# Seven-product FFN tiles: one 512-column matmul where two 256-column matmuls shared a weight half

## The chip, the cores and the metric

The kernel runs on one core of a Trainium2 chip. The metric is device time in microseconds (us) of one execution; lower is better. A core has TensorE (PE in the profile: matmul, PEld: weight load), VectorE (DVE), ScalarE (ACT), GpSimd (POOL) and SyncE (SP), each with its own queue of instructions, and 16 DMA engines.

## The reference, cut to what matters

One decoder layer on 512 tokens of width 2048: a mixer half (RMSNorm, an input projection, four groups of mixers, an output projection, residual), then a gated MLP, residual, and a final RMSNorm. The change lies in the first matmul of the MLP:

```python
def conv_gated_mlp(h, w_up, w_dw, b_dw, w_down):
    up = h @ w_up                          # (512, 2048) @ (2048, 11008)
    gate, val = jnp.split(up, 2, axis=-1)  # 5504 columns each: 43 tiles of 128
    gate = causal_dwconv(gate, w_dw, b_dw) # width 3
    return (jax.nn.gelu(gate, approximate=True) * val) @ w_down
```

All is float32, and the matmul units are fed with two-part numbers: `hi` is the value rounded to the matmul's format (float32r), `lo` what is left. A product is then hi·hi + hi·lo + lo·hi, three matmuls.

## The kernel before, in words

The work is transposed: a result tile has 128 columns of the weight as its partitions and tokens along its free dimension. `FFN` has 43 tiles `f` of 128 gate columns and the 128 value columns that belong to them. The first three are done plainly (`ffn_std`). The other 40 are done in `ffn_up` by a scheme of the Strassen kind: gate and value, the two halves of the 2048 inputs and the two halves of the 512 tokens make a 2x2x2 product, for which seven products of half the tokens do instead of eight. The seven weight forms of a tile are `a`, `b`, `d` (blocks of the weight as they are), `r1`, `r2`, `r3`, `r4` (sums of blocks); the seven forms of the input lie in the tiles `X0` to `X7`, each `[128, 7, 2, 256]`: form, hi or lo, 256 tokens.

`ffn_up` goes through a list `seq` of products. For each tile from `f` = 4 on the order is: `a` of `f`, `d` of `f`-1, `r1` of `f`, `r4` of `f`-1, `r2` of `f`, `b` of `f`, `r3` of `f`. I call these seven in a row one round. For entry `k` of the list the code writes, in this order:

- `load(k + 6)`: weight blocks from memory by SP's queue (`a`, `b`, `d`); for `r1` and `r3` a block by SP and a second one added to it by a DMA of POOL's queue.
- `stage(k + 2)`: for `r2` and `r4` a sum on VectorE; then the split of the 128x1024 weight form: a ScalarE cast to `hi` (tile `uh...`) and a VectorE subtraction for `lo` (tile `ul...`). The pool `wq` has three buffers for each, so the cast of one product waits for the end of the product three places before.
- `product(k)`: for each of eight input tiles, weight `hi` with input `hi`, weight `hi` with input `lo`, weight `lo` with input `hi`, all into the same 256 columns of a PSUM bank.
- `after(k)`: what the result of the product is used for. Bank "a" of a tile takes `a`, then `r2`, then `r3`, then `d` on top of one another, and bank "r1" takes `r1`, then `r4`. A partial sum that is needed must therefore be read before the next product is added: after `a` and `r2` a copy on ScalarE (tiles `A12`/`A13`), after `r3` a copy to `A14`, to which VectorE adds bank "r1". After `r4` follows the chain that finishes the tile: VectorE makes the gate `g` (`A8`/`A9`), multiplies it by the RMSNorm factor (`rstd`, `A15`), ScalarE and VectorE do the convolution and the gelu into `c` (`A10`/`A11`), VectorE multiplies by the value parts (bank "a" and `A14`), and `keep` sends `c` to memory by SP's queue.

The order on PE is that of the code. On the other queues the builder's scheduler sets the order by its own estimate of the times, with `load` and `stage` raised in priority; once built, each engine takes its instructions in that fixed order.

Of the kernel before, what the change touches and what calls it, by code (L numbers as in the profile page):

```python
# [8 lines left out]
F32 = mybir.dt.float32  # L9
# [4 lines left out]
ADD, SUB, MUL = ALU.add, ALU.subtract, ALU.mult  # L14

P = 128
# [32 lines left out]
class Kernel:  # L49
# [988 lines left out]
    def tail(self):  # L1038
        tc = self.tc
        self.mp.release()  # L1040
        self.ap.release()
        fx = tc.alloc_tile_pool(name="fx", bufs=1, reuse_waits="tile")
        ft = tc.alloc_tile_pool(name="ft", bufs=1, reuse_waits="tile")
        ft2 = tc.alloc_tile_pool(name="ft2", bufs=2, reuse_waits="tile")
        self.x2d = [self.dr.tile([P, 1024], F32, name=f"x2d{p}") for p in range(8)]
        self.tp = ft
        self.acc = self.tmp("rstd", pool=self.cp)
        self.xf = []
        for q in range(4):
            ps = self.quad(q, (0, 2), 0)  # L1050
            for o in range(4):
                x = self.x2[4 * q + o]
                self.tt(x, x, ps[o], ADD)
            for p in (2 * q, 2 * q + 1):
                self.forms1(fx, p)
            for p in (2 * q, 2 * q + 1):
                self.square2(p, ft2)
        self.ffn_std()
        ft2.release()
        ft.release()  # L1060
        self.ffn_up(self.xf, self.rp, self.rs)
        for pool in (fx, self.aq, self.rp):
            pool.release()
        with tc.tile_pool(name="sr", bufs=1, side="right", reuse_waits="tile") as sr, \
                tc.tile_pool(name="sr2", bufs=2, side="right", reuse_waits="tile") as sr2, \
                tc.tile_pool(name="xp", bufs=1, reuse_waits="tile") as xp, \
                tc.tile_pool(name="sp", bufs=1, reuse_waits="tile") as sp, \
                tc.tile_pool(name="dp", bufs=1, reuse_waits="tile") as dp, \
                tc.tile_pool(name="dp2", bufs=2, reuse_waits="tile") as dp2:
            self.tp, self.xp, self.sp, self.sr = dp, xp, sp, sr  # L1070
            base_tmp = self.tmp
            self.tmp = lambda tag, w=512, dt=F32, pool=None: base_tmp(tag, w, dt, pool or {"sq": dp2, "av": sr2}.get(tag))
            self.down()
# [91 lines left out]

    def ffn_up(self, xf, rp, rstd):
        tc, nc, a = self.tc, self.nc, self.a
        IX = {"a": 0, "b": 1, "r4": 2, "r1": 3, "r2": 4, "r3": 5, "d": 6}  # L1170
        seq = [(NSTD, x) for x in ("a", "r1", "r2", "b", "r3")]
        for f in range(NSTD + 1, NF + 1):
            for form, back in (("a", 0), ("d", 1), ("r1", 0), ("r4", 1), ("r2", 0), ("b", 0), ("r3", 0)):
                if f - back < NF:
                    seq.append((f - back, form))
        raws, staged = {}, {}
        blk = self.blk
        v8 = lambda t: t.rearrange("p (k c)->p k c", k=8)

        def raw(f, form):  # L1180
            pool = self.wp if form == "d" else rp
            t = pool.tile([P, 1024], F32, tag="raw", name=f"u{form}_{f}")
            raws[f, form] = t
            return t

        def load(k):
            if k >= len(seq):
                return
            f, form = seq[k]
            if form in ("a", "b", "d"):  # L1190
                nc.sync.dma_start(v8(raw(f, form)), blk(f, form))
            elif form in ("r1", "r3"):
                t = raw(f, form)
                nc.sync.dma_start(v8(t), blk(f, "c"))
                nc.gpsimd.dma_start(v8(t), blk(f, "d" if form == "r1" else "a"), accum_op=ADD)  # L1195

        def stage(k):
            if k >= len(seq) or k in staged:
                return
            f, form = seq[k]  # L1200
            if form == "r2":
                self.tt(raw(f, form), raws[f, "r1"], raws[f, "a"], ADD)
            if form == "r4":
                self.tt(raw(f, form), raws[f, "r2"], raws[f, "b"], ADD)
            hi = self.wq.tile([P, 1024], F32R, tag="hi", name=f"uh{form}_{f}")
            lo = self.wq.tile([P, 1024], F32R, tag="lo", name=f"ul{form}_{f}")
            self.split_to(hi, lo, raws[f, form])
            staged[k] = (hi, lo)

        bank, sv = {}, {}  # L1210

        def product(k):
            f, form = seq[k]
            wh, wl = staged.pop(k)
            new = form in ("a", "b", "r1")
            if new:
                bank[f, form] = self.pa() if form == "b" else self.pb() if f % 2 else self.pa()
            ps = bank[f, {"a": "a", "r2": "a", "r3": "a", "d": "a", "b": "b", "r1": "r1", "r4": "r1"}[form]]
            for p in range(8):
                x, c = xf[p][:, IX[form]], slice(p * P, p * P + P)  # L1220
                self.mm(ps[:, 0:256], wh[:, c], x[:, 0], new and p == 0, False, True)
                self.mm(ps[:, 0:256], wh[:, c], x[:, 1], False, False, True)
                self.mm(ps[:, 0:256], wl[:, c], x[:, 0], False, p == 7, True)

        def after(k):
            f, form = seq[k]
            if form == "a":
                sv[f, "s"] = self.at(12 + f % 2, F32)
                nc.scalar.copy(sv[f, "s"][:, 0:256], bank[f, "a"][:, 0:256])
            elif form == "r2":  # L1230
                nc.scalar.copy(sv[f, "s"][:, 256:512], bank[f, "a"][:, 0:256])
            elif form == "r3":
                sv[f, "w"] = w = self.at(14, F32)[:, 0:256]
                nc.scalar.copy(w, bank[f, "a"][:, 0:256])
                self.tt(w, bank[f, "r1"][:, 0:256], w, ADD)
            elif form == "b":
                sv[f, "g"] = self.at(8 + f % 2, F32)
                self.tt(sv[f, "g"][:, 0:256], bank[f, "b"][:, 0:256], sv[f, "s"][:, 0:256], ADD)
            elif form == "r4":
                g, c = sv[f, "g"], self.at(10 + f % 2, F32)  # L1240
                self.tt(g[:, 256:512], bank[f, "r1"][:, 0:256], sv[f, "s"][:, 256:512], ADD)
                self.tt(g, g, rstd, MUL)
                self.conv_gelu(f, g, c)
                self.stt(c, c, -1.0, rstd, MUL, MUL)
                self.tt(c[:, 0:256], bank[f, "a"][:, 0:256], c[:, 0:256], MUL)
                self.tt(c[:, 256:512], sv[f, "w"], c[:, 256:512], MUL)
                self.keep(f, c)

        LD, AH = 6, 2
        for k in range(LD):  # L1250
            with tc.high_priority(self.hp):
                load(k)
        for k in range(AH):
            with tc.high_priority(self.hp):
                stage(k)
        for k in range(len(seq)):
            with tc.high_priority(self.hp):
                load(k + LD)
                stage(k + AH)
            product(k)  # L1260
            after(k)
# [195 lines left out]
```

## Time and profile before

| | |
|---|---|
| median of 3 runs | 1925.88 us (1922.14 to 1925.94) |
| profiled execution, its own time | 1925.42 us |
| its span in the profile | 1923.6 us |
| busy: PE, PEld, DVE, ACT, POOL | 98%, 88%, 68%, 42%, 9% |
| stage of the 40 seven-product tiles | about 619 to 1431 us |
| chain that ended last, on PE | 89% |
| DMA, mean over the span | 153 GB/s |

Busy time is the share of the span in which an engine had an instruction at work; matmuls overlap each other, so a busy PE is not yet a PE at its peak. The chain is followed back from the last instruction to what released each step. PEclk is the clock that was granted to TensorE, as a share of full speed. In the rows of the profile buffer numbers are left out: `pa` and `pb` are PSUM banks, `uhr`/`ulr` are hi and lo of any of `r1` to `r4`, `A` any of `A8` to `A15`. L96 is the matmul helper, L59 and L62 the VectorE helpers, L105 the cast of a split, L72 an activation.

### The profile page before, as it was taken

The page shows a single profiled execution, that of the slowest core. Times are in us where ns is not written, and L with a number is a line of the kernel's source. Part 1 is how long each engine was busy: PE and PEld are TensorE (multiplying, and loading weights), DVE is VectorE, ACT ScalarE, POOL GpSimd, SP SyncE. Part 2 cuts the span into 40 slices and gives each one's busy share as a digit, 9 for nine tenths or more (in the row PEclk, how much of TensorE's full clock was granted, in tenths as well). Part 3 has the DMA queues.
Part 4 walks back from the last instruction along what each step waited for, and adds up shares of the span by engine and source line. Part 5 has one row for each costly group of instructions (what it writes and reads, how often), then busy time and mean ns, then how long its engine had stood idle before and what let it go on. Part 6 is the DMA issues. An engine that isn't in the chain of part 4 may idle for free.

```text
span 1923.6 us, 29377 instructions
## 1 busy us (share of the span) xinstructions
PE 1875.6 (98%) x11662; PEld 1683.5 (88%) x11662; DVE 1313.1 (68%) x1978; ACT 808.5 (42%) x1054; POOL 164.5 (9%) x243
## 2 busy tenths in 40 slices
PE   8999999999999999999999999999999999999996
PEld 6788887888777999999999999999988888888886
DVE  8699989999683776777767767777774333333334
ACT  6323446432662444544444444444453222222332
POOL 6210020202000000000000000000000000000000
PEclk9999999999999999999999999999999999999998
DMA  5232332533335777777777777777748343333324
GB/s 203 89 96 91 102 93 79 168 102 92 120 125 181 200 195 208 186 194 199 194 211 181 197 202 189 210 186 194 196 126 271 116 139 109 116 110 96 97 95 152
DMA packets 104251, 293.87 MB, mean 153 GB/s; under 512 B 14960, under 2 KB 21104, under 8 KB 104112
## 3 DMA queue, kind: packets, MB, share of 16 engines
q1 hardware_dynamic: 91200, 248.20, 38.7%
q0 software_dynamic: 12624, 43.26, 13.6%
q8 instruction: 91, 1.49, 0.3%
q10 hardware_dynamic: 288, 0.52, 0.1%
q14 instruction: 48, 0.39, 0.1%
HBM read 269.79 MB, written 19.66 MB: 150 GB/s over the span
## 4 chain that ended last, share of the span: by engine, by line
PE 89%; DVE 6%; DMA 2%; ACT 2%; issue 1%; POOL 0%; DVEq 0%; SPq 0%; ACTq 0%; POOLq 0%
PE pa L96 57%; PE pb L96 31%; DVE lo L59 1%; DMA ur<-w_up 1%; ACT hi L105 1%; DVE X L59 1%; DMA av<-act 1%; DVE M L59 0%; DVE bk L59 0%; DMA raw<-w_dnt 0%; ACT L72 0%; DVE l_x L62 0%; DVE A L59 0%; DVE pr L59 0%; DVE A L62 0%
## 5 line engine op out<-in xcount | busy, mean ns | idle before, releaser
L96 PE MATMUL pa<-A,hi 128*128 128x512 f32 x1312 | 414.5, 398 | 14.9 <-ACT A L72 7.3
L59 DVE TENSOR_TENSOR lo<-raw,hi 128x1024 fp32r<-128x1024 f32 (+1 forms) x187 | 231.0, 1236 | 275.9 <-ACT hi L105 275.7
L105 ACT CAST hi<-raw 128x1024 fp32r<-128x1024 f32 (+1 forms) x187 | 195.6, 1047 | 503.9 <-PE pa L96 423.9
L96 PEld LDWEIGHTS pa<-A,hi 128*128 128x128 f32 x1312 | 247.7, 191 | 74.4 <-ACT A L72 7.7
L105 ACT CAST uhr<-ur 128x1024 fp32r<-128x1024 f32 x160 | 167.6, 1047 | 262.0 <-PE pb L96 129.0
L59 DVE TENSOR_TENSOR ulr<-ur,uhr 128x1024 fp32r<-128x1024 f32 x160 | 195.5, 1222 | 116.9 <-ACT uhr L105 116.9
L96 PE MATMUL pa<-A,lo 128*128 128x512 f32 x656 | 258.9, 398 | 2.9 <-DVE lo L59 2.9
L96 PE MATMUL pb<-X,uhr 128*128 128x256 f32 x1280 | 233.9, 283 | 2.0 <-ACT uhr L105 2.0
L96 PE MATMUL pa<-X,uhr 128*128 128x256 f32 x1280 | 233.8, 283 | 0.0
L96 PEld LDWEIGHTS pb<-X,uhr 128*128 128x128 f32 x1280 | 199.7, 192 | 2.2 <-ACT uhr L105 2.2
L96 PEld LDWEIGHTS pa<-X,uhr 128*128 128x128 f32 x1280 | 199.7, 192 | 0.0
L96 PE MATMUL pb<-X,ulr 128*128 128x256 f32 x640 | 181.2, 283 | 0.8 <-DVE ulr L59 0.8
L96 PE MATMUL pa<-X,ulr 128*128 128x256 f32 x640 | 181.1, 283 | 0.0
L96 PEld LDWEIGHTS pa<-A,lo 128*128 128x128 f32 x656 | 124.9, 191 | 32.4 <-DVE lo L59 3.8
L96 PE MATMUL pa<-Sh,hi 128*128 128x512 f32 (+1 forms) x392 | 149.6, 382 | 2.9 <-DVE A L59 2.9
L96 PE MATMUL pa<-Sh,lo 128*128 128x512 f32 (+1 forms) x392 | 149.3, 381 | 0.0
L96 PE MATMUL pa<-Sl,hi 128*128 128x512 f32 (+1 forms) x392 | 149.1, 380 | 0.0
L1195 POOL DMA_DIRECT2D ur<-w_up x80 | 69.9, 874 | 838.7 <-DMA ur<-w_up 276.8
L96 PE MATMUL pb<-Sh,hi 128*128 128x512 f32 (+1 forms) x328 | 125.3, 382 | 0.0
L96 PE MATMUL pb<-Sh,lo 128*128 128x512 f32 (+1 forms) x328 | 125.1, 381 | 0.0
L96 PE MATMUL pb<-Sl,hi 128*128 128x512 f32 (+1 forms) x328 | 124.9, 381 | 0.0
L96 PEld LDWEIGHTS pb<-X,ulr 128*128 128x128 f32 x640 | 122.9, 192 | 1.0 <-DVE ulr L59 1.0
(295 smaller groups left out, 3524.3 us busy)
## 6 DMA issues: line engine op xcount, KB each, us to landing
ur<-w_up SPq DMA_DIRECT2D x80, 512.0 KB, 6.7
ur<-w_up POOLq DMA_DIRECT2D x80, 512.0 KB, 7.9
raw<-w_dn SPq DMA_DIRECT2D x54, 512.0 KB, 3.6
raw<-w_b SPq DMA_DIRECT2D x40, 512.0 KB, 3.7
ud<-w_up SPq DMA_DIRECT2D x40, 512.0 KB, 8.2
ua<-w_up SPq DMA_DIRECT2D x40, 512.0 KB, 6.8
ub<-w_up SPq DMA_DIRECT2D x40, 512.0 KB, 3.7
raw<-w_out SPq DMA_DIRECT2D x32, 512.0 KB, 3.6
```

The lines of the kernel that those rows point to most:

```text
L59: (eng or self.nc.vector).tensor_tensor(out, x, y, op=op)
L96: self.nc.tensor.matmul(ps, lhsT=l, rhs=r, start=start, stop=stop, skip_group_check=go_on)
L105: self.nc.scalar.copy(hi, src)
L1195: nc.gpsimd.dma_start(v8(t), blk(f, "d" if form == "r1" else "a"), accum_op=ADD)
```

## The change

The two matmuls with the same weight half become one of 512 columns: input hi and lo lie side by side in `X`, so weight `hi` meets both at once. Columns 0 to 255 of the bank then hold hi·hi, columns 256 to 511 hold hi·lo, and weight `lo` with input `hi` is added to the latter. Each partial result has now two halves that must still be added. This is done on VectorE, two quarters at a time, in two new tiles of a new pool `ub` with one buffer each: `ut` (for the gate) and `uv` (for the value), each `[128, 2, 2, 256]`.

```diff
-                self.mm(ps[:, 0:256], wh[:, c], x[:, 0], new and p == 0, False, True)
-                self.mm(ps[:, 0:256], wh[:, c], x[:, 1], False, False, True)
-                self.mm(ps[:, 0:256], wl[:, c], x[:, 0], False, p == 7, True)
+                self.mm(ps, wh[:, c], x.rearrange("p n c->p (n c)"), new and p == 0, False, True)
+                self.mm(ps[:, 256:512], wl[:, c], x[:, 0], False, p == 7, True)
+
+        two = lambda t: t.rearrange("p (n c)->p n c", n=2)
+        quad = lambda tag, f: ub.tile([P, 2, 2, 256], F32, tag=tag, name=f"{tag}_{f}")

         def after(k):
             f, form = seq[k]
             if form == "a":
                 sv[f, "s"] = self.at(12 + f % 2, F32)
-                nc.scalar.copy(sv[f, "s"][:, 0:256], bank[f, "a"][:, 0:256])
+                nc.scalar.copy(sv[f, "s"], bank[f, "a"])
             elif form == "r2":
-                nc.scalar.copy(sv[f, "s"][:, 256:512], bank[f, "a"][:, 0:256])
+                sv[f, "u"] = self.at(14, F32)
+                nc.scalar.copy(sv[f, "u"], bank[f, "a"])
             elif form == "r3":
-                sv[f, "w"] = w = self.at(14, F32)[:, 0:256]
-                nc.scalar.copy(w, bank[f, "a"][:, 0:256])
-                self.tt(w, bank[f, "r1"][:, 0:256], w, ADD)
+                sv[f, "v"] = v = quad("uv", f)
+                nc.scalar.copy(v[:, 1], two(bank[f, "a"]))
+                self.tt(v[:, 1], two(bank[f, "r1"]), v[:, 1], ADD)
             elif form == "b":
-                sv[f, "g"] = self.at(8 + f % 2, F32)
-                self.tt(sv[f, "g"][:, 0:256], bank[f, "b"][:, 0:256], sv[f, "s"][:, 0:256], ADD)
+                sv[f, "t"] = quad("ut", f)
+                self.tt(sv[f, "t"][:, 0], two(bank[f, "b"]), two(sv[f, "s"]), ADD)
+            elif form == "d":
+                v = sv[f, "v"]
+                nc.scalar.copy(v[:, 0], two(bank[f, "a"]))
+                self.tt(v[:, :, 0], v[:, :, 0], v[:, :, 1], ADD)
             elif form == "r4":
-                g, c = sv[f, "g"], self.at(10 + f % 2, F32)
-                self.tt(g[:, 256:512], bank[f, "r1"][:, 0:256], sv[f, "s"][:, 256:512], ADD)
+                t, v, g, c = sv[f, "t"], sv[f, "v"], self.at(8 + f % 2, F32), self.at(10 + f % 2, F32)
+                self.tt(t[:, 1], two(bank[f, "r1"]), two(sv[f, "u"]), ADD)
+                self.tt(two(g), t[:, :, 0], t[:, :, 1], ADD)
                 self.tt(g, g, rstd, MUL)
                 self.conv_gelu(f, g, c)
                 self.stt(c, c, -1.0, rstd, MUL, MUL)
-                self.tt(c[:, 0:256], bank[f, "a"][:, 0:256], c[:, 0:256], MUL)
-                self.tt(c[:, 256:512], sv[f, "w"], c[:, 256:512], MUL)
+                self.tt(two(c), v[:, :, 0], two(c), MUL)
                 self.keep(f, c)
```

In `tail` the pool `ub` is opened before `ffn_up` and closed after it. Nothing else is edited. The scheduler orders the queues of the stage anew. In the rows below the digits after a tile's name are its tile `f` and a running number, and a wait names the engine whose semaphore is waited for.

On PE the round of `f` = 22, at the step from `a` of 22 to `d` of 21, read before:

```order
L96 MATMUL pa694_9904<-X7_4972,ula_22_9834 128x256
L96 MATMUL pb687_9669<-X0_4693,uhd_21_9866 128x256 [waits Activation_49]
L96 MATMUL pb687_9669<-X0_4693,uhd_21_9866 128x256
L96 MATMUL pb687_9669<-X0_4693,uld_21_9867 128x256 [waits DVE_49]
L96 MATMUL pb687_9669<-X1_4698,uhd_21_9866 128x256 x2
```

and reads now:

```order
L96 MATMUL pa693_8932<-X7_4972,uha_22_8877 128x512
L96 MATMUL pa693_8932<-X7_4972,ula_22_8878 128x256
L96 MATMUL pb686_8749<-X0_4693,uhd_21_8902 128x512 [waits Activation_49]
L96 MATMUL pb686_8749<-X0_4693,uld_21_8903 128x256 [waits DVE_49]
L96 MATMUL pb686_8749<-X1_4698,uhd_21_8902 128x512
```

In both, `d` goes to the bank that `r3` of 21 was added to, and its first matmul waits for ScalarE.

On ScalarE, the same place in the round before (L1234 is the copy after `r3` of 21, L1229 the copy after `a` of 22):

```order
L105 CAST uhr1_22_9900<-ur1_22_9761 128x1024 [waits DMASW7_49,PE_49]
L1234 COPY A14_693_9894<-pb687_9669 128x256 [waits DVE_49,PE_49]
L105 CAST uhr4_21_9935<-ur4_21_9933 128x1024 [waits PE_49,Activation_49]
L1229 COPY A12_695_9929<-pa694_9904 128x256 [waits PE_49]
L105 CAST uhr2_22_9967<-ur2_22_9965 128x1024 [waits PE_49,Activation_49]
```

and now (L1240 is the copy after `r3` of 21, L1234 that after `a` of 22, L1247 the new one after `d` of 21, L72 the gelu of 20):

```order
L105 CAST uhr1_22_8928<-ur1_22_8819 128x1024 [waits DMASW7_49,PE_49,Activation_49]
L72 ACTIVATE A10_690_8843<-A10_690_8843 128x512 [waits DVE_49,Activation_49]
L105 CAST uhr4_21_8955<-ur4_21_8953 128x1024 [waits PE_49]
L1234 COPY A12_694_8949<-pa693_8932 128x512 [waits PE_49]
L1240 COPY uv_21_8922<-pb686_8749 128x512 [waits DVE_49]
L105 CAST uhr2_22_8981<-ur2_22_8979 128x1024 [waits PE_49,Activation_49]
L1247 COPY uv_21_8922<-pb686_8749 128x512 [waits PE_49]
```

The copy after `r3` stood ahead of the cast for `r4` and of the copy after `a`; it now stands behind both.

On VectorE, the end of the chain of tile 20 before (the two products into `A10`, then the sum into `A14` that follows the copy after `r3` of 21):

```order
L62 SCALAR_TENSOR_TENSOR A10_690_9792<-A10_690_9792,A15_538_4991 128x512 [waits Activation_49]
L59 TENSOR_TENSOR uld_21_9867<-ud_21_9728,uhd_21_9866 128x1024 [waits DMAHW5_49,Activation_49]
L59 TENSOR_TENSOR A10_690_9792<-pa680_9434,A10_690_9792 128x256 [waits DVE_49]
L59 TENSOR_TENSOR A10_690_9792<-A14_686_9659,A10_690_9792 128x256
L59 TENSOR_TENSOR ulr1_22_9901<-ur1_22_9761,uhr1_22_9900 128x1024 [waits PE_49,Activation_49]
L59 TENSOR_TENSOR A14_693_9894<-pb689_9736,A14_693_9894 128x256 [waits Activation_49]
L59 TENSOR_TENSOR ulr4_21_9936<-ur4_21_9933,uhr4_21_9935 128x1024 [waits PE_49,Activation_49]
```

and now (the product with `uv_20` is the last step of tile 20, and the last reader of that buffer):

```order
L62 SCALAR_TENSOR_TENSOR A10_690_8843<-A8_689_8842,par_84,A10_690_8843 128x510 [waits DVE_49]
L59 TENSOR_TENSOR ulr1_22_8929<-ur1_22_8819,uhr1_22_8928 128x1024 [waits PE_49,Activation_49]
L62 SCALAR_TENSOR_TENSOR A10_690_8843<-A10_690_8843,A15_538_4991 128x512 [waits Activation_49]
L59 TENSOR_TENSOR ulr4_21_8956<-ur4_21_8953,uhr4_21_8955 128x1024 [waits PE_49,Activation_49]
L59 TENSOR_TENSOR A10_690_8843<-uv_20_8739,A10_690_8843 128x512 [waits DVE_49]
L59 TENSOR_TENSOR uv_21_8922<-pb688_8802,uv_21_8922 128x512 [waits Activation_49]
L59 TENSOR_TENSOR ulr2_22_8982<-ur2_22_8979,uhr2_22_8981 128x1024 [waits PE_49,Activation_49]
```

The last product of tile 20 stood ahead of the subtractions for `r1` of 22 and `r4` of 21; it now stands behind both. On ScalarE this order holds in the rounds of `f` = 5 to 42 and on VectorE in those of 5 to 41; in round 42 the last product of tile 40 stands ahead of the subtraction for `r4` of 41. On SP only the stores of finished tiles move, by two places, and on POOL nothing moves.

More of the change, by code (lines that the diff above doesn't have):

```diff
@@ L1060, in tail @@
         ft.release()
-        self.ffn_up(self.xf, self.rp, self.rs)
-        for pool in (fx, self.aq, self.rp):
+        ub = tc.alloc_tile_pool(name="ub", bufs=1, reuse_waits="tile")
+        self.ffn_up(self.xf, self.rp, self.rs, ub)
+        for pool in (ub, fx, self.aq, self.rp):
             pool.release()
@@ L1161, in keep, with ffn_up @@
         self.actd.append(t)
-    def ffn_up(self, xf, rp, rstd):
+    def ffn_up(self, xf, rp, rstd, ub):
         tc, nc, a = self.tc, self.nc, self.a
```

## The prediction

> **What bounds the kernel now.** I read the page's busy times first, then its slices.
>
> ```profile
> PE 1875.6 (98%) x11662; PEld 1683.5 (88%) x11662; DVE 1313.1 (68%) x1978; ACT 808.5 (42%) x1054; POOL 164.5 (9%) x243
> ...
> PE   8999999999999999999999999999999999999996
> PEld 6788887888777999999999999999988888888886
> DVE  8699989999683776777767767777774333333334
> ...
> PEclk9999999999999999999999999999999999999998
> ```
>
> TensorE has hardly a gap, and the stage of seven products (slices 13 to 30) has none. So the price of a product is the spacing of its matmuls. The busy times by stage give the spacings, and two products read out in order of time give the shape (columns of the stage rows: window, its length, PE, PEld, DVE, ACT, POOL busy, clock, DMA share, GB/s).
>
> ```profile
> 1000.00:1200.00 200.00, 200.00 (x1669) 200.00 (x1669) 147.03 (x178) 96.93 (x120) 17.29 (x20) 1.00 0.74 197
> ...
> 1600.00:1800.00 200.00, 200.00 (x881) 165.16 (x881) 66.00 (x71) 49.24 (x56) 0.00 (x0) 1.00 0.33 102
> ```
>
> ```profile
> 1000.06 0.40 PE L96 MATMUL pa<-X,uha 128*128 128x256 f32 x2
> ...
> 1002.82 0.28 PE L96 MATMUL pa<-X,ula 128*128 128x256 f32 x1
> 1002.94 0.40 PE L96 MATMUL pb<-X,uhd 128*128 128x256 f32 x2
> ```
>
> A product is 24 matmuls of 256 columns in 1002.94 - 1000.06 = 2.88 us: 120 ns each, and no wait between `a` and `d`. A round of seven takes 20.16 us, 40 of them 806 us. In the later stage, where all matmuls have 512 columns, the spacing is 200/881 = 227 ns: less than twice 120, so a matmul carries about 13 ns beside its columns.
>
> **The matmuls.** Per input tile, three matmuls (360 ns) become one of 512 and one of 256 (227 + 120 = 347 ns). That is 13 ns for 40 x 7 x 8 = 2240 input tiles: -29 us. No row mixes the widths; the bounds are 0 (360 ns stay) and 40 ns for each input tile (the 512 at the price of 320 - 120 = 200), -90 us. I take the spacings as they stand. A product becomes 2.78 us, a round 19.4 us. The Trainium skill ("TensorE: Matmul & The Clock Gate", Back-to-back issue gap) gives N/2.4 + 2.5 ns for an isolated gap, by which a matmul saved would be worth 2.5 ns and the term -6 us; the rows here say 120 ns where this gives 109, so I keep the rows.
>
> **The added work on VectorE and ScalarE.**
>
> ```profile
> L59 DVE TENSOR_TENSOR A<-pa,A 128x256 f32<-128x256 f32 x100 | 42.0, 420 | 12.7 <-PE pa L96 12.5
> L59 DVE TENSOR_TENSOR x<-x,pa 128x512 f32<-128x512 f32 x48 | 32.3, 682 | 1.1 <-PE pa L96 0.8
> ...
> L1229 ACT COPY A<-pa 128x256 f32<-128x256 f32 x20 | 7.3, 366 | 0.0
> L242 ACT COPY A<-pb x1: 586/586/586, 568.9 to 568.9; 128x512 f32<-128x512 f32 x1
> ```
>
> For each tile three sums widen (682 - 420 = 0.26 us each), two sums of 512 are new, and one product of 0.68 replaces two of 0.42: 0.79 + 1.36 - 0.16 = +2.0 us on VectorE. From 147/200 x 20.16 = 14.8 us a round it goes to 16.8 of 19.4 us: 87%, still not the bound. ScalarE gains 3 x 0.22 + 0.59 = 1.2 us on 9.8. As mere load I cost both at nothing: TensorE's 19.4 us a round hide them. DMA moves the same bytes (share 0.74, at 19.4 us at most 0.77); the stores that move on SP wait for a product that a store waited for before, and the loads behind them are issued six products, 6 x 2.78 = 16.7 us, ahead. The order is another matter.
>
> **The new wait.** `d` adds to the bank that `r3` of its tile left, so it must wait for the copy after `r3`. By the new order that copy stands on ScalarE behind the cast for `r4` and the copy after `a`. The cast needs a buffer that frees when `a` ends, and `a` ends exactly where `d` should begin. So the copy cannot run before `d` is due. It has a second condition: its target `uv` has one buffer, whose last reader is the final product of the tile before, and this stands on VectorE behind the subtraction for `r4`, which needs the same cast. The chain from the end of `a`, priced by rows of before:
>
> ```profile
> 1003.08 1.05 ACT L105 CAST uhr<-ur 128x1024 fp32r<-128x1024 f32 x1 [1.24 <-PE pa L96]
> 1004.03 0.37 ACT L1229 COPY A<-pa 128x256 f32<-128x256 f32 x1
> ...
> 1001.29 1.22 DVE L59 TENSOR_TENSOR ulr<-ur,uhr 128x1024 fp32r<-128x1024 f32 x1
> 1002.42 0.42 DVE L59 TENSOR_TENSOR A<-pb,A 128x256 f32<-128x256 f32 x1
> 1004.16 1.23 DVE L59 TENSOR_TENSOR ulr<-ur,uhr 128x1024 fp32r<-128x1024 f32 x1 [1.31 <-ACT uhr L105]
> 1012.24 0.69 DVE L59 TENSOR_TENSOR A<-A,A 128x512 f32<-128x512 f32 x1
> 1021.12 0.42 DVE L59 TENSOR_TENSOR A<-A,A 128x256 f32<-128x256 f32 x1
> 1021.63 0.38 ACT L1234 COPY A<-pa 128x256 f32<-128x256 f32 x1 [0.27 <-DVE A L59]
> ```
>
> - end of `a` to cast: 1003.08 - 1002.94 = 0.14
> - cast to the start of its subtraction: 1004.16 - 1003.08 = 1.08
> - subtraction to the next VectorE instruction: 1002.42 - 1001.29 = 1.13
> - the final product, 128x512: 0.69
> - its end to the copy that waited for it: 1021.63 - 1021.54 = 0.09
> - the copy from the bank, 128x512: 0.59
> - copy to matmul: 0.05, from the rows below
>
> That is 3.77 us by which `d` starts late. ScalarE's own queue alone (cast, copy after `a`, copy after `r3`: 0.14 + 0.95 + about 0.55, a little under its own time, + 0.59 + 0.05) would give 2.3 us, the lower bound. The other inputs are earlier. In VectorE's new queue the subtraction for `r1` starts 0.14 + 1.08 = 1.22 us after the start of `a` (the twelve instructions from the sum after `r4` to it take about 9.4 of the 8.3 + 1.2 us there are), and the multiplication by the norm behind it ends at 1.22 + 1.13 + 0.68 = 3.0; the subtraction for `r4` can start only at 2.78 + 1.22 = 4.0. And the later products find their halves split: each has two products' time for a cast and a subtraction (2.2 us). So nothing pays the wait back. The last tile of before, where `r3` and `d` are neighbours, shows that `d` does wait for such a copy behind a cast:
>
> ```profile
> 1423.50 1.04 ACT L105 CAST hi<-raw 128x1024 fp32r<-128x1024 f32 x1 [1.83 <-PE pa L96]
> 1424.45 0.37 ACT L1234 COPY A<-pa 128x256 f32<-128x256 f32 x1
> ...
> 1423.30 0.28 PE L96 MATMUL pa<-X,ulr 128*128 128x256 f32 x1
> 1424.87 0.50 PE L96 MATMUL pa<-X,uhd 128*128 128x256 f32 x2 [1.29 <-ACT A L1234]
> ```
>
> The copy ended at 1424.82, `d` started at 1424.87, 1.45 us after the 1423.42 at which it was due. In the new order 37 rounds (`d` of 4 to 40) have the whole chain: 139.5 us. `d` of 41 has ScalarE's part, 2.3, and `d` of 42 about 0.6 more than its 1.45 (its copy now also waits for a product of VectorE). Together +142 us.
>
> **The clock after the wait.** A row of 3.4 us each, at three stalls of before:
>
> ```profile
> core 0: us, PE busy (x), PEclk, DMA share, GB/s
> 497.40:500.80 3.40, 1.81 (x7) 1.00 0.24 43
> 500.80:504.20 3.40, 2.88 (x7) 0.53 0.30 114
> ...
> 623.70:627.10 3.40, 1.79 (x12) 1.00 1.04 229
> 627.10:630.50 3.40, 3.40 (x31) 1.00 0.84 295
> ...
> 1436.10:1439.50 3.40, 0.78 (x3) 1.00 0.71 236
> 1439.50:1442.90 3.40, 3.40 (x10) 0.52 0.45 144
> ```
>
> The clock goes in steps of 3.4 us: where TensorE was busy 0.78 or 1.81 of them, the next 3.4 us run at half clock; at 1.79 elsewhere not. So the limit lies near 1.6 us of idle in a step. A wait of 3.77 us leaves 3.6 us idle (the last matmul runs 0.16 into it), spread over two steps. If the first has under 1.6 of it (1.6 of 3.4 positions), the second has over 2.0, and the step after runs at half clock, full of work: 1.7 us lost. If both have over 1.6 (0.4 of 3.4), about 2.5. If the first has over 2.0 (1.4 of 3.4), the half step begins in the idle time: 0.9 to 1.6, mean 1.25. Mean 0.80 + 0.29 + 0.51 = 1.6 us; the ends are 0 and 2.5. Times 37, and about 1 for `d` of 41: +60 us.
>
> The Trainium skill (same page, HAM oscillation — how this bites in real kernels) says that idle gaps over about 3.4 us, a whole window of its monitor, bring half clock. By that this term would be near 4 us in place of 60. The trace here differs: the idle time that ended at 1438.72 was 2.93 us. It stays as a rival.
>
> **The hand-over to the next stage.**
>
> ```profile
> 1438.72 0.50 PE L96 MATMUL pa<-Sh,hi 128*128 128x512 f32 x1 [2.93 <-DVE A L59]
> ```
>
> Before, the next stage's last banks wait for the final product of tile 42, which reads bank "a": 2.9 us, and 1.7 us of half clock behind it (1439.50 above). Now a copy empties that bank earlier, but bank "r1" is read behind splits of the next stage. Between 0 and -4.6 us; I take -3, since the copy has no long chain ahead of it.
>
> **The sum.** -29 + 142 + 60 - 3 = +170 us on the profiled execution's 1925.4: 2095 us. The median of the runs is 0.5 above it: 2096.
>
> **The rivals.**
>
> - Half clock only after a wholly idle step. 3.6 us of idle cover a whole step of 3.4 in 0.2/3.4 = 6% of positions: 37 x 0.06 x 1.7 = 4 us in place of 60, 2040. For it speaks the row at 623.70, where two gaps of a step did nothing; against it 500.80 and 1439.50. 13%. (The Trainium skill's rule above is of this kind.)
> - The shorter wait: if VectorE's final product comes ahead in time of what I worked out, ScalarE's queue alone holds `d` by 2.3 us, 2.1 of them idle; with the limit above two positions in three bring a half step, 1.15 us on average. 37 x (2.3 + 1.15) = 128 in place of 199: 2025. Against it: the subtraction for `r4` has no way past the cast. 8%.
> - Faster: `d` doesn't wait, because the copy after `r3` gets done during `a`, for instance since the order of the built program doesn't hold on the chip. Then -29 - 3: 1893. It decides at a copy done 3.8 us earlier than I have it. The order of before is found in its trace instruction by instruction, so 5%.
> - VectorE's 87% turns into a further wait behind each round, or both steps fall under the limit each time (37 x 2.5 = 92): 2128 or a little more. 9%.
>
> My forecast keeps 65%. The range takes in the shorter wait and the double step: 2022 to 2132. A measurement of this kernel tells about 0.2% from no change; faster 0.05, within it 0.01, slower 0.94.
>
> **What will show it.** Right: the waits list has TensorE waiting for the L1240 copy, about 37 times and 3.6 us each, some 135 us; rows of matmuls 347 ns apart in pairs between; a clock of about 0.93 in the stage, which takes some 980 us; `d` alone starts late. Wrong: no such wait (then the order or the bank's reuse was misread), a clock of 1.00, pairs at 360 ns, or TensorE waiting for VectorE's splits.

## The result, and the profile after

The changed kernel takes 2115.59 us (median of 4 runs, 2114.25 to 2120.2) where the kernel before takes 1924.91 us (4 runs, 1922.14 to 1925.94): a ratio of 1.1001, 95% interval 1.0984 to 1.1019, or 191 us more. The forecast was 2096 us within 2022 to 2132. The direction and the mechanism were right; the size was 20 us short, and the experiments below find in which term.

The page of the changed kernel, busy times and two of the slices:

```profile
PE 1935.1 (92%) x9422; PEld 1621.8 (77%) x9422; DVE 1394.0 (66%) x2018; ACT 851.2 (40%) x1094; POOL 167.1 (8%) x243
...
PE   8999999999998888888888888888889999999997
...
PEclk9999999999999889999999999888999999999998
```

TensorE has 2240 matmuls fewer and is busy for longer: part of its work now runs at half clock. Its row of slices, full before, has 8s through the stage of seven products, slices 13 to 30. The list of waits (what waited, for what: us in all, times, longest) says what is in them:

```profile
PE pa L96 <- ACT uv L1240: 68.2, 20, 3.5
PE pb L96 <- ACT uv L1240: 65.0, 19, 3.5
```

The windows of the stage, with the columns as in the prediction:

```profile
800.00:1000.00 200.00, 172.01 (x878) 147.51 (x877) 132.84 (x150) 84.36 (x103) 14.00 (x16) 0.90 0.59 157
1000.00:1200.00 200.00, 172.00 (x886) 147.78 (x885) 133.58 (x151) 85.28 (x104) 13.54 (x16) 0.91 0.58 157
```

TensorE waits 39 times, 133.2 us, for the copy after `r3` (L1240). VectorE is busy 67% of the stage and ScalarE 42%: neither is the bound by its load. Here is one wait in order of time, on all engines, from the changed kernel's trace:

```profile
1013.16 0.28 PE L96 MATMUL pb<-X,ula 128*128 128x256 f32 x1
...
1013.36 1.05 ACT L105 CAST uhr<-ur 128x1024 fp32r<-128x1024 f32 x1 [0.62 <-PE pb L96]
1014.31 0.58 ACT L1234 COPY A<-pb 128x512 f32<-128x512 f32 x1
1014.44 1.23 DVE L59 TENSOR_TENSOR ulr<-ur,uhr 128x1024 fp32r<-128x1024 f32 x1 [0.69 <-ACT uhr L105]
1015.58 0.68 DVE L59 TENSOR_TENSOR A<-uv,A 128x512 f32<-128x512 f32 x1
...
1016.30 0.59 ACT L1240 COPY uv<-pa 128x512 f32<-128x512 f32 x1 [1.41 <-DVE A L59]
...
1016.94 0.59 PE L96 MATMUL pa<-X,uhd 128*128 128x512 f32 x1 [3.50 <-ACT uv L1240]
...
1017.54 0.63 PE L96 MATMUL pa<-X,uhd 128*128 128x512 f32 x1
...
1018.18 0.63 PE L96 MATMUL pa<-X,uhd 128*128 128x512 f32 x1
```

`a` ends at 1013.16 + 0.12 = 1013.28, the spacing of a 256-column matmul after its start. Cast for `r4`, its subtraction, final product of the tile before, copy after `r3`, `d`: each row begins where the one ahead of it releases it, and `d` is 1016.94 - 1013.28 = 3.66 us late. Behind it come pairs of a 512- and a 256-column matmul 0.64 us apart (1017.54 to 1018.18) in place of 0.35: half clock.

The full waits run from the first to the last of these two rows, 37 of them:

```profile
662.40 0.79 PE L96 MATMUL pa<-X,uhd 128*128 128x512 f32 x1 [3.50 <-ACT uv L1240]
...
1574.23 0.79 PE L96 MATMUL pa<-X,uhd 128*128 128x512 f32 x1 [3.50 <-ACT uv L1240]
```

A round takes 911.83/36 = 25.33 us. At full clock the pairs of this trace are 349 ns apart on the mean (1908 of them). So 7 x 8 pairs are 19.57 us of the round, the wait is 3.66, and 2.10 us are left for the clock, where the forecast had 1.6.

### The profile page after: what moved, and what is told of

It is laid out like the page before. It is cut to its first block, busy times and chain, and to the rows that moved or that the text cites. A ratio compares the mean times of both kernels' runs of the same rounds, so it can differ in the third digit from the quotient of the medians.

```text
span 2112.9 us, 24908 instructions
## 1 busy us (share of the span) xinstructions
PE 1935.1 (92%) x9422; PEld 1621.8 (77%) x9422; DVE 1394.0 (66%) x2018; ACT 851.2 (40%) x1094; POOL 167.1 (8%) x243
## 4 chain that ended last, share of the span: by engine, by line
PE 84%; DVE 8%; ACT 4%; DMA 2%; issue 1%; SPq 0%; DVEq 0%; ACTq 0%; POOLq 0%
PE pa L96 54%; PE pb L96 30%; DVE ulr L59 2%; ACT uhr L105 2%; DVE A L59 1%; DVE lo L59 1%; ACT uv L1240 1%; DMA ur<-w_up 1%; ACT hi L105 0%; DMA raw<-w_a 0%; DVE M L59 0%; DVE X L59 0%; DMA raw<-w_dnt 0%; DMA par<-par 0%; DVE bk L59 0%
## 5 line engine op out<-in xcount | busy, mean ns | idle before, releaser
L96 PE MATMUL pb<-X,uhr 128*128 128x512 f32 x640 | 229.8, 398 | 1.0 <-ACT uhr L105 1.0
L96 PE MATMUL pa<-X,uhr 128*128 128x512 f32 x640 | 229.2, 397 | 0.0
L96 PE MATMUL pa<-X,uhd 128*128 128x512 f32 x160 | 95.2, 602 | 68.2 <-ACT uv L1240 68.2
L96 PE MATMUL pb<-X,uhd 128*128 128x512 f32 x160 | 90.6, 577 | 65.0 <-ACT uv L1240 65.0
L96 PEld LDWEIGHTS pb<-X,uhr 128*128 128x128 f32 x640 | 122.1, 191 | 30.2 <-ACT uhr L105 1.4
L96 PEld LDWEIGHTS pa<-X,uhr 128*128 128x128 f32 x640 | 121.5, 190 | 28.8
```

The source lines that it names most:

```text
L96: self.nc.tensor.matmul(ps, lhsT=l, rhs=r, start=start, stop=stop, skip_group_check=go_on)
```

## The experiments

Two questions stood: does the wait (and the clock behind it) hold the whole loss, with the matmuls and the added sums as forecast; and what sets the loss of clock, which came out too large?

**1. The wide matmul alone.** The kernel before, with the two matmuls made one and everything else left.

```diff
 (against the kernel before)
-                self.mm(ps[:, 0:256], wh[:, c], x[:, 0], new and p == 0, False, True)
-                self.mm(ps[:, 0:256], wh[:, c], x[:, 1], False, False, True)
-                self.mm(ps[:, 0:256], wl[:, c], x[:, 0], False, p == 7, True)
+                self.mm(ps, wh[:, c], x.rearrange("p n c->p (n c)"), new and p == 0, False, True)
+                self.mm(ps[:, 256:512], wl[:, c], x[:, 0], False, p == 7, True)
```

> The matmuls of the change with all the rest as before: the partial sums read columns 0 to 255 alone, so hi times lo and lo times hi are left out of the 40 tiles. The queues of ScalarE and VectorE keep the order of before. Theory (the matmuls gain 13 ns for each input tile, all the loss comes from the new wait and its clock): no wait ahead of d, clock 1.00 in the stage, pairs of matmuls 346 ns apart, 1925 - 30 = 1895 us, perhaps 4 less at the end of the stage. Rival A (the mixed widths themselves cost time or lower the clock): over 1925 us, clock under 0.97 in the stage.

Measured: 1905.66 us (1894.48 to 1912.52) beside 1921.93 for the kernel before; ratio 0.9897, interval 0.9866 to 0.9928. The stage has no gap and full clock:

```profile
1000.00:1200.00 200.00, 200.00 (x1134) 173.38 (x1133) 149.28 (x181) 98.08 (x121) 17.48 (x20) 1.00 0.75 200
```

So the wide matmul gains, and makes no wait. The four runs lie apart: two at 1912.5, the others at 1894.5 and 1898.9. The profiled one, at 1912.5, has pairs of 2 x 200/1134 = 353 ns, where those of number 3 below are 2 x 200/1156 = 346; 2240 x 7 ns are 16 us, about the difference between the runs. No trace of the two shorter ones is on record, so that they ran at 346 is not shown. What makes one execution run at 346 and another at 353, both at a granted clock of 1.00, stays open.

**2. The new sums and their order, without the wide matmul.** The changed kernel, with three 256-column matmuls into the two halves.

```diff
-                self.mm(ps, wh[:, c], x.rearrange("p n c->p (n c)"), new and p == 0, False, True)
+                self.mm(ps[:, 0:256], wh[:, c], x[:, 0], new and p == 0, False, True)
+                self.mm(ps[:, 256:512], wh[:, c], x[:, 1], False, False, True)
```

> The change without its wide matmul: three matmuls of 256 columns as before, but into the two halves of the bank, and the new sums on VectorE in the order of the changed kernel. Theory: the wait ahead of d stays at 3.5 us of idle, 37 times; the gain of the matmuls is missing, so 2116 + 30 = 2146 us, give or take 8 for another phase of the clock's steps. Rival A (the wide matmul lowers the clock or sets the wait): near the time of before plus the small added sums, under 1960 us.

Measured: 2085.13 us (2081.39 to 2089.55); ratio 1.0851, interval 1.0837 to 1.0865. The waits are the same in number and length (the list of waits, then the stage's window):

```profile
PE pa L96 <- ACT uv L1241: 68.1, 20, 3.5
PE pb L96 <- ACT uv L1241: 64.9, 19, 3.5
```

```profile
1000.00:1200.00 200.00, 172.02 (x1363) 170.40 (x1362) 137.91 (x156) 85.93 (x105) 13.97 (x16) 0.96 0.60 161
```

So the loss comes from the sums and their order, not from the matmul. But the time missed the expectation by 61 us: from the same 133 us of waiting this kernel lost only some 31 us of clock, the changed kernel 76. Both are counted from the stretches of half clock in the traces: 70.8 and 167.8 us of them, idle time left out. The work of an input tile takes 640 ns there in both kernels, where it takes 360 and 349 at full clock, so 44% and 45% of that time are lost. That the clock costs a fixed sum behind each wait is thereby wrong.

**3. The wait removed, all else kept.** The chain runs through `uv`, whose one buffer is free only after the final product. Here the sum of its halves goes to a tile of its own, so that `uv` is free right after `d`; the scheduler then puts the copy after `r3` behind the cast for `r1`, ahead of the cast for `r4`.

```diff
-                self.tt(v[:, :, 0], v[:, :, 0], v[:, :, 1], ADD)
+                sv[f, "w"] = ub.tile([P, S], F32, tag="uw", name=f"uw_{f}")
+                self.tt(two(sv[f, "w"]), v[:, :, 0], v[:, :, 1], ADD)
...
-                self.tt(two(c), v[:, :, 0], two(c), MUL)
+                self.tt(c, sv[f, "w"], c, MUL)
```

> The changed kernel with one edit: the finished value half is summed into a tile of its own, so that the buffer of uv is free right after d and not only after the final product of the tile. By the built order the copy after r3 then stands right behind the cast for r1, ahead of the cast for r4 and of the copy after a. Theory: the wait ahead of d is gone, the clock stays at 1.00 in the stage, and the matmuls' gain shows: 1893 us (1888 to 1898), faster than both. Rival B (VectorE's added sums bound the round once the wait is away): waits of TensorE for VectorE's splits, 1925 us or more.

Measured: 1891.5 us (6 runs, 1889.98 to 1905.88) beside 1921.93; ratio 0.9863, interval 0.9837 to 0.9888. One tile of 256 KB more (128 x 512 x 4 bytes) takes 224 us off the changed kernel and makes it faster than the kernel before. The stage, and ScalarE's rows in one round:

```profile
1000.00:1200.00 200.00, 200.00 (x1156) 176.34 (x1155) 173.86 (x197) 109.04 (x134) 18.03 (x21) 1.00 0.76 203
```

```profile
1007.05 1.05 ACT L105 CAST uhr<-ur 128x1024 fp32r<-128x1024 f32 x1 [1.72 <-PE pa L96]
1008.01 0.58 ACT L1240 COPY uv<-pa 128x512 f32<-128x512 f32 x1
1008.52 0.63 ACT L72 ACTIVATE A<-A 128x512 f32<-128x512 f32 x1
1009.78 1.05 ACT L105 CAST uhr<-ur 128x1024 fp32r<-128x1024 f32 x1 [0.63 <-PE pb L96]
1010.74 0.58 ACT L1234 COPY A<-pb 128x512 f32<-128x512 f32 x1
```

The copy into `uv` now stands 1.77 us ahead of the cast for `r4`, not behind it. VectorE is busy 87% of the stage, all the added sums included, and TensorE 100%: the sums are hidden.

**4. The wait filled with work.** Fifteen matmuls of 512 columns into a spare bank ahead of `d`: `d` comes as late as before, but TensorE is not idle.

```diff
+            if form == "d" and f < NF - 1:
+                spare = self.pb()
+                for i in range(FILL):      # 15
+                    self.mm(spare, xf[0][:, 0, 0, 0:128], xf[0][:, 0].rearrange("p n c->p (n c)"), i == 0, i == FILL - 1)
```

> The changed kernel, and 15 matmuls of 512 columns into a bank of their own ahead of each d from tile 3 to 41: 15 x 227 ns = 3.4 us of TensorE work in the 3.67 us in which it waits anyway. Their result is used by nothing. Theory (half clock comes from TensorE's idle steps, 2.3 us in each of 37 rounds): clock 1.00 in the stage, d starts 3.7 us late as before, and the time falls by 37 x 2.3 = 85 us to about 2030 us though work is added. Rival C (the clock is lowered by something else in this stage, or the lost 2.3 us are not the clock's): about 2116 us, clock still near 0.90.

Measured: 2050.9 us (2048.18 to 2051.62); ratio 1.0669, interval 1.0656 to 1.0683. With work added the kernel is 65 us faster than the changed one:

```profile
1000.00:1200.00 200.00, 199.50 (x1084) 169.22 (x1083) 145.24 (x164) 91.57 (x111) 14.21 (x17) 1.00 0.63 165
```

Full clock and hardly any idle time: of the 191 us, at least 65 hang on the clock and not on the lateness. The lateness alone would be 2115.6 - 76 = 2040; of the 11 us above that, 2240 x 4 = 9 are the wider spacing of this execution (353 ns, where the changed kernel's had 349).

**5. The shorter wait.** Number 3, with the copy after `r3` forced behind the copy after `a`: only ScalarE's queue holds `d`.

```diff
 (against number 3; third(f) is written after "a" of f + 1)
+        def third(f):
+            v = sv[f, "v"]
+            if f < NF - 1:
+                nc.scalar.copy(v[:, 1, 0, 0:1], sv[f + 1, "s"][:, 0:1])
+            nc.scalar.copy(v[:, 1], two(bank[f, "a"]))
+            self.tt(v[:, 1], two(bank[f, "r1"]), v[:, 1], ADD)
```

> The kernel with a sum tile of its own (1891.5 us), in which the copy after r3 is made to follow the copy after a on ScalarE (a copy of one column between them forces it; its value is written over). So ScalarE's queue holds d, and VectorE's final product does not. By the changed kernel's own rows: 0.14 + 0.95 + 0.48 + 0.2 + 0.59 + 0.05 = 2.4 us from the end of a to d, 2.25 of it idle, in 38 rounds: +92 us, and of the 3.4 us steps of the clock about half bring a half step, 0.9 us a round, +33: 2016 us (1985 to 2035). Rival D (the wait of 3.67 us is VectorE's, ScalarE's order alone costs little): idle under 1 us a round, under 1930 us.

Measured: 2053.01 us (2052.9 to 2058.85); ratio 1.0681, interval 1.066 to 1.0701.

```profile
PE pb L96 <- ACT uv L1234: 46.9, 20, 2.3
PE pa L96 <- ACT uv L1234: 46.0, 20, 2.4
```

```profile
1000.00:1200.00 200.00, 181.24 (x969) 156.14 (x968) 144.90 (x164) 93.21 (x119) 14.88 (x17) 0.94 0.62 164
```

TensorE idles for 92.9/40 = 2.3 us a round (list of waits, and the window behind it), which makes `d` 2.5 us late; 0.2 of that is the added copy of one column, and the other 2.3 are what the prediction's bound from below said. The time lies above the 1985 to 2035 that were expected: the clock lost some 54 us in 35 half-clock steps, where 33 us were expected. If the waits fell evenly on the steps of the clock, about 25 of the 40 would leave over 1.8 us idle in one step; here 35 brought half clock. The rest of the miss fits the longer wait and a mean spacing of 350 ns.

**6. The added sums alone.** Number 3's sums on three 256-column matmuls: no wide matmul and no wait.

```diff
 (number 3 with the edit of number 2)
```

> The kernel with a sum tile of its own, but with the three matmuls of 256 columns: only the added sums of VectorE and copies of ScalarE are left of the change. Theory (they lie beside TensorE's work at no cost): the time of before within 5 us, perhaps 4 less at the end of the stage; no wait of TensorE in the rounds. Rival B (they cost): 2 us in each of 40 rounds, about 2000 us.

Measured: 1918.69 us (1916.48 to 1920.77) beside 1922.66; ratio 0.9976, interval 0.9964 to 0.9989. The added work on VectorE and ScalarE costs nothing that shows. The 4 us gained fit the hand-over to the next stage: TensorE's 2.9 us wait there is no longer in the list. With the added work, VectorE is at 84% of the stage:

```profile
1000.00:1200.00 200.00, 200.00 (x1669) 200.00 (x1668) 167.32 (x189) 104.10 (x128) 17.53 (x20) 1.00 0.74 197
```

**7. The wait half filled.** As number 4 with eight matmuls, so that 62.8/38 = 1.65 us of idle time are left in a round.

```diff
-                for i in range(FILL):      # 15
+                for i in range(FILL):      # 8
```

> The changed kernel with 8 instead of 15 added matmuls ahead of d: TensorE idles for 3.67 - 8 x 0.23 - 0.16 = 1.7 us in a round. Theory (a full-clock step of 3.4 us brings half clock only where it holds 1.95 us or more of idle, as the rows of the run with narrow matmuls show it): clock 1.00 in the stage, 2031 us, or 2050 where the matmul pairs run 353 ns apart as in the run with 15. Rival E (the limit lies near 1.6 us, as I had put it before): half steps in about a tenth of the rounds, some 5 us more; rival F (idle time in any amount lowers the clock): clock under 0.95, over 2070 us.

Measured: 2043.92 us (2042.89 to 2051.0); ratio 1.0634, interval 1.0611 to 1.0657, between the two times expected without half clock. Not one half-clock step lies in the stage, with its 38 waits (the list of waits, then the stage's window):

```profile
PE pa L97 <- ACT uv L1245: 33.3, 20, 1.7
PE pb L97 <- ACT uv L1245: 29.5, 18, 1.7
```

```profile
1000.00:1200.00 200.00, 186.80 (x1026) 158.59 (x1024) 145.91 (x165) 92.35 (x112) 14.90 (x17) 1.00 0.63 167
```

So up to 1.65 us in a step cost only themselves. And the clock goes by what TensorE does in the wait, not by the lateness of `d`, which is the same as ever.

**8. The round of the changed kernel made seven steps long.** In all these traces the granted clock changes only at multiples of 3.413 us from one another; I call these stretches the clock's steps. In number 2 a round without half clock takes 23.91 us, 7.005 steps. The theory then was that such a round keeps its place against the steps. Four matmuls ahead of `r1`, outside the wait, make the changed kernel's round 23.04 + 0.95 = 23.99 us, 7.03 steps.

```diff
+            if form == "r1" and f > NSTD:
+                spare = self.pb()
+                for i in range(FILL):      # 4
+                    self.mm(spare, xf[0][:, 0, 0, 0:128], xf[0][:, 0].rearrange("p n c->p (n c)"), i == 0, i == FILL - 1)
```

> The changed kernel with 4 added matmuls of 512 columns (0.92 us) after d, where nothing waits: the wait stays, the round at full clock becomes 23.02 + 0.92 = 23.94 us, seven steps of 3.41 us (23.89). Theory (what the clock costs hangs on how the idle time falls on the steps; at seven steps a round it falls on nearly the same place each time, for many rounds on 1.6 + 1.9 us where no step is lowered): added work 37 us, clock loss down from 2.3 us a round to about 0.7, -59: 2094 us, faster than the changed kernel with more work. Rival G (matmuls of 512 columns lower the clock more than those of 256 at the same idle time, whatever the round's length): 2116 + 37 = 2153 us.

Measured: 2155.06 us (2149.77 to 2158.89); ratio 1.1198, interval 1.1169 to 1.1226: the changed kernel's time and the 37 us of added work, 57 half-clock steps in the stage where that has 54, and the same clock:

```profile
1000.00:1200.00 200.00, 172.04 (x866) 146.63 (x865) 126.10 (x142) 80.47 (x98) 14.00 (x16) 0.90 0.57 154
```

Taken alone this spoke for the rival: that 256-column matmuls lose less clock than 512-column ones.

**9. The round of number 2 made longer than seven steps.** The same four matmuls in number 2, which tells the two apart again.

```diff
 (number 2 with the edit of number 8)
```

> The kernel of three 256-column matmuls with the new sums and their order, with four extra 512-column matmuls ahead of r1 in every round of the stage, after d (work added: 39 x 4 x about 0.237 us = 37 us). Its round without half clock was 23.91 us, 7.005 of the 3.413 us steps of the clock, so an idle time of 3.5 us that once fell as 1.6 + 1.9 us on two steps, without half clock, fell so again in the next rounds; with 0.95 us more it is 24.86 us, 7.28 steps, and the split moves on by 0.28 of a step each round. The wait ahead of d stays 3.5 us, 39 times, by both. Theory (the small loss of clock in the narrow kernel came from the length of its round, which held the split): the loss rises from about 35 us to some 75 to 85, as in the kernel of the change: 2085 + 37 + 45 = 2167 us (2150 to 2178), clock near 0.91 to 0.93 in the stage. Rival (256-column matmuls lose less clock at the same idle time, whatever the length of the round): the loss stays near 35 us: 2085 + 37 = 2122 us (2110 to 2135), clock near 0.96.

Measured: 2188.14 us (2183.66 to 2190.48); ratio 1.1383, interval 1.1364 to 1.1402. That is 103 us more than number 2 for 37 us of added work, with 256-column matmuls as there: the rival is out, and what is left is the length of the round. The size was missed upward (2150 to 2178 expected). The half clock costs some 85 us, counted as in number 2, and two rows twenty rounds apart show how it comes to so much:

```profile
1066.94 0.58 PE L97 MATMUL pb<-X,uhd 128*128 128x256 f32 x1 [3.50 <-ACT uv L1246]
...
1613.07 0.58 PE L97 MATMUL pb<-X,uhd 128*128 128x256 f32 x1 [3.50 <-ACT uv L1246]
```

546.13/20 = 27.306 us, 8.000 steps. The round is 24.86 us without half clock, and stretches by half clock until it is eight steps long; there it stays. 68 half-clock steps lie in its stage, two in most rounds.

### The clock, step by step

Windows laid on the clock's own steps of 3.41 us show what decides (window, its length, PE busy with count, PEclk, DMA share, GB/s). First two rounds of the changed kernel:

```profile
682.70:686.12 3.42, 1.19 (x8) 1.00 0.73 174
686.12:689.53 3.41, 2.15 (x7) 0.50 1.00 284
689.53:692.94 3.41, 3.41 (x12) 0.50 0.60 231
692.94:696.36 3.42, 3.42 (x21) 1.00 0.53 95
757.80:761.21 3.41, 2.77 (x16) 1.00 0.86 208
761.21:764.62 3.41, 0.54 (x3) 1.00 0.78 162
764.62:768.04 3.42, 3.42 (x12) 0.50 1.01 352
768.04:771.45 3.41, 3.41 (x21) 1.00 0.61 120
```

The idle time of a step is its length less PE busy. At 757.80 it falls as 0.64 + 2.87: one half step follows, full of work; at 640 ns a pair in place of 349 it loses 45% of 3.41 us, 1.55 us. At 682.70 it falls as 2.23 + 1.26, and there are two half steps: the second follows on 1.26 us of idle in a step that was itself at half clock. Now number 2, two rounds:

```profile
1272.92:1276.34 3.42, 1.73 (x15) 1.00 0.93 181
1276.34:1279.75 3.41, 1.60 (x13) 1.00 0.90 215
1279.75:1283.16 3.41, 3.41 (x30) 1.00 0.79 297
1296.82:1300.23 3.41, 1.75 (x15) 1.00 0.74 173
1300.23:1303.64 3.41, 1.58 (x13) 1.00 1.03 262
1303.64:1307.06 3.42, 3.42 (x18) 0.50 0.66 262
```

1.69 + 1.81 us of idle time, and nothing happens; the next round has 1.66 + 1.83, and a half step follows. I counted every whole step of the stages of six kernels (the changed one and numbers 2, 5, 7, 8, 9) in the record of the granted clock. Of the steps at full clock with under 1.7 us idle none of 1308 was followed by half clock, among them 35 with 1.6 to 1.7; with 1.7 to 1.9 it was 6 of 46; with 1.9 and more all 160. Of the steps at half clock with under 0.59 us idle none of 166 was followed by another; with 0.59 or more all 71 were.

In idle time there are thus two limits, near 1.8 us (between 1.76 and 1.84 the rows go both ways) and near 0.6. The 1.95 us expected for number 7 were too high. But idle time need not be what the clock goes by. Count the columns of the matmuls instead, each matmul's spread over its spacing (227 and 120 ns for 512 and 256 columns at full clock, 427 and 213 at half). All 71 half-clock steps with half clock behind them then held under 3200 columns, and all 166 others held more; at full clock 165 of the 166 with half clock behind them held under 3200, and 1343 of the 1348 others more. A full-clock step without idle holds some 7500. So one limit on the work done in a step fits the same steps as two limits on its idle time, since at half clock the same busy time does less work. No run here tells these two readings apart.

By the limits in idle time 3.50 us of idle cost nothing only where they fall as 1.67 to 1.83 and the rest, a place 0.16 us wide out of 3.41. Number 2's round moves by 23.91 - 23.89 = 0.02 us against the steps, so once it is in that place it stays there for three to six rounds: 19 of its 37 full waits brought no half clock. Number 8's moves by 0.1, and none of its waits fell there. That the width of the place is what kept number 8 out is worked out from these numbers and wasn't tried by itself.

The Trainium skill ("TensorE: Matmul & The Clock Gate", Part 1: The HAM clock gate) has the window free-running and 3413 ns long; 27.306 us for eight of them agrees. The Trainium skill's section HAM oscillation — how this bites in real kernels, on the same page, warns of idle gaps over about 3.4 us; here gaps of 2.3 us (number 5) brought 35 half steps, and gaps of 1.65 us (number 7) none. The measurement decides.

## Why the prediction was right or wrong, point by point

- **The matmuls** (-29): right in kind, within a spread of 16 us between executions that the forecast didn't have. Three matmuls took 360 ns; pairs take 346 in number 3 (2240 x 13.5 ns are -30), 353 in number 1, and 349 on the mean in the changed kernel, about -24. Number 1 shows the gain by itself.
- **The added sums** (0, hidden): right. Number 6 is not slower than the kernel before, and number 3 has VectorE at the 87% of the forecast with TensorE full.
- **The new wait** (3.77 us, 37 times, +142): right in cause, place, count and size. Its seven parts measured 0.08, 1.08, 1.14, 0.68, 0.04, 0.59 and 0.05, 3.66 us. With the two shorter ones at the end of the stage (`d` of 41 and 42) it is about 37 x 3.66 + 2.6 = +138. Number 3 removes it by a buffer, and the loss goes with it; number 5 gives the forecast's lower bound of 2.3 us when only ScalarE's queue is left in the chain.
- **The clock after the wait** (+60): the mis-sized term. It measured about 76 us: 54 half steps, 184.3 us long with 16.5 us of idle time in them, and 45% of the other 167.8 lost. The step that failed is "the limit lies near 1.6 us of idle in a step", used for the second step as for the first ("if both have over 1.6"). It was read from windows that lay some 0.2 us beside the clock's steps. Laid on the steps, the same two places of the kernel before read:

```profile
497.57:500.99 3.42, 1.64 (x6) 1.00 0.29 60
500.99:504.40 3.41, 3.08 (x7) 0.50 0.25 96
620.45:623.87 3.42, 2.11 (x18) 1.00 1.07 223
623.87:627.28 3.41, 1.97 (x14) 1.00 1.03 234
627.28:630.69 3.41, 3.41 (x30) 1.00 0.82 290
```

  So 1.78 us of idle brought half clock, and 1.31 and 1.44 did not; the 1.59 and 1.61 us between which the forecast drew its line are in no step. By the rows of the six kernels the limit is 1.8 us for a step at full clock and 0.6 for one that runs at half clock already.

  The case with two half steps is therefore not 0.4 of 3.4 positions but 2.90 - 1.83 = 1.07 of them. A half step full of work costs 1.55 us, not 1.7. An even fall of the waits then gives 1.67 positions at 1.55 us, 1.07 at 2.58 and 0.51 at 1.39, which is 1.78 us a round or 66 us. Most of the other 10 are in the second assumption, that the waits fall evenly on all positions: 16 of the 37 brought two half steps and 21 one, where an even fall gives about 12 and 24. The rival with two falls each time (2128) missed by less than the forecast did, but by luck: its condition, "both steps fall under the limit each time", isn't what the rows show.
- **The hand-over** (-3): about right. The 2.9 us wait of TensorE for the final product of tile 42 isn't in the list of waits any more, and number 6, which has the same end of the stage, gained 4.0 us (by its interval 2.1 to 6.9).
- **The sum:** -24 + 138 + 76 - 4 = +186, where the span went from 1923.6 to 2112.9, +189; the 3 us between them are assigned to nothing.
- **The rivals:** half clock only after a wholly idle step is refuted by number 5, whose waits of 2.3 us can't cover a step and lost 54 us of clock. The shorter wait and no wait at all are both real, but in kernels with another order: numbers 5 and 3.

## What to carry to other kernels

A tile with one buffer ties its first writer to the last reader of the round before; with engines that take their instructions in a fixed order this can close a chain through three engines, so before widening a result look for what the writer will stand behind, and spend one more buffer there (224 us here). When TensorE must wait, idle time of up to 1.7 us in a clock step cost only itself here, and 1.9 us or more brought at least one step at half clock behind it, 1.55 us when full of work: filling half of the wait with work that nobody reads saved 72 us (number 7). In a loop with a wait in each round the loss of clock can depend on the round's length in clock steps (numbers 2 and 9), so an edit that has nothing to do with the wait can move the time by tens of microseconds.

## What the runs showed of the hardware that was not expected

- About 1.8 us of idle in a 3.41 us step bring half clock, and in a half-clock step 0.6 us are enough to stay there; one limit of some 3200 columns of matmul work in a step fits both.
- At half clock a pair takes 640 ns where it takes 349 at full clock, 1.83 times as long and not twice.
- A round can lock to the clock: number 9's took 8.000 steps, twenty rounds in a row, and the kernel 66 us more than number 2 and the added work.
- A 512-column and a 256-column matmul with a weight load each take 346 ns in one execution (number 3) and 353 in others (numbers 1, 4 and 7), at the same granted clock, 16 us for 2240 pairs; the cause is open.
